# Norm steps of a two-layer decoder: one set of small operations for three token tiles, a shorter Newton step, a later fold, four lead units ahead of a norm

## The chip, the cores and the metric

The program runs on one core of one Trainium2 chip. Its metric is the time of one execution in microseconds on the device; the figures shown are the runs of the kernel before, and one further execution of it was profiled.

## The reference, cut to what matters

One inference step of a two-layer decoder with 1024 prompt tokens and 64 sample tokens (8 sequences of 8). Every layer is a mixer followed by a squared-ReLU MLP, and every one of these four sublayers has a norm in front and a norm behind:

```
def rmsnorm(x, g):
    xf = x.astype(jnp.float32)
    y = xf * lax.rsqrt(jnp.mean(xf * xf, axis=-1, keepdims=True) + EPS) * g.astype(jnp.float32)
    return y.astype(x.dtype)
...
    for l in range(DEPTH):
        h = rmsnorm(x, g_mix_pre[l])
        ...   # layer 0: m = pooling and short-convolution mixer; layer 1: m = (u * spatial(rmsnorm(v))) @ w_out_c
        x = x + rmsnorm(m, g_mix_post[l])
        h = rmsnorm(x, g_ffn_pre[l])
        f = jnp.square(jax.nn.relu(h @ w_up[l])) @ w_down[l]
        x = x + rmsnorm(f, g_ffn_post[l])
```

D_MODEL is 1024, the hidden size of the MLP 4096. Everything is float32.

## The kernel before, in words

**Products.** A float32 product is made of three products of rounded halves (`mm3`, L294 to L296): each operand is split into a rounded part and the rest (`hh` and `hl` of an activation, a cast on ACT at L116 and a subtraction on DVE at L117 of a weight tile `w` from its raw copy). Such three matmuls are called a triple here. A unit of an up projection is eight triples.

**Chunks.** The 1088 tokens are handled as three chunks: chunk 0 and chunk 1 of 384 prompt tokens (three tiles of 128), chunk 2 of 320 (256 prompt, 64 sample). Work runs over them in the order 2, 0, 1 (`ORD`). Chunk 2 is kept with features on the partitions, chunks 0 and 1 with tokens on the partitions.

**A boundary** is what lies between two sublayers: the norm behind, the residual add, the norm in front, and the halves `hh`, `hl` that the next products read. There are three boundaries in mid-program (here b1 at about 303 to 363 us between the first mixer and its MLP, b2 at about 1053 to 1113 us between that MLP and the second mixer, b3 at about 1386 to 1446 us between the second mixer and its MLP), a start that has only the norm in front, and a tail that has only the norm behind.

**Chunk 2's boundary** (`boundary`, `pre_tile`, `pre_end`): the sum of squares over partitions is made by a transposition on DVE, a reduction `red`, a matmul with a matrix `fold` on PE (`rstat`, L334 to L339), and a root with a Newton step (`rsqrt_small`). The first such fold belongs to the norm behind; after it eight tiles each are scaled (`acc`, L545, half on DVE and half on POOL), added to `x` (L554), split (`hh` L369 on ACT, `hl` L370 on DVE) and squared (L363 on ACT, L364 on POOL). The second fold (below: fold 2) gives the factor `rb` of the norm in front, which is applied only behind the up product (L878).

**Chunk 0's and chunk 1's boundary** (`boundary_tok`, `normed`): the sum of squares of the sublayer's output arrives in `ss` (squared on ACT at L470 as the last adds L467 are made); then for each of three token tiles: L431 adds two halves, `rsqrt_small` takes root and Newton step on a column of 128 x 1, L433 multiplies by it and the gain, L434 adds to `x`, ACT squares `x` with its sum (L415), a second `rsqrt_small` on 128 x 1, and ACT scales (L417). `arrive` then transposes the three tiles on PE (L454) and makes `hh` (L457, ACT) and `hl` (L458, DVE), eight of each.

**Order.** The boundaries are generators in a list `bg`; `pump(k)` advances it by k steps after each product (`E_STEPS` 3 in the last block of a sublayer, `U_STEPS` 7 between units), and a yielded number (`FOLD_GAP`) holds a generator until that many microseconds of products, by a count the program keeps, have been issued. A scheduler then fixes the order on each engine; each engine works its own list in that order. The last block of a sublayer has 24 triples of 512 columns for chunk 0 and 24 for chunk 1. The first four up units (`LEAD`, the lead units) are done for chunk 2, then for chunk 0, then for chunk 1. The rows of `x` that stay are written to memory by DMAs that ACT issues (L441), the outputs at the tail by DMAs that SP issues (L436).

## Time and profile before

| | us |
|---|---|
| three runs | 2178.21, 2180.25, 2180.49 (median 2180.25) |
| profiled execution | 2179.24 |
| its span | 2177.0 |
| PE busy | 2113.6 (97%) |
| DVE busy | 1275.7 (59%) |
| ACT busy | 689.5 (32%) |
| POOL busy | 73.0 (3%) |

The profiled execution lies 1.0 us under the median of the three runs, and its time is 2.2 us more than the span of its instructions. PE is TensorE's matmuls, DVE VectorE, ACT ScalarE, POOL GpSimd, SP SyncE. In a timeline row the first number is the start, the second the duration, and a bracket at the end gives the idle time just before and what ended it.

### The profile page before, as it was taken

To read this page: it belongs to the slowest core of one execution; us is meant where nothing else is said; L and a number is where in the kernel's file an instruction comes from. 1 tells how busy PE (TensorE), PEld (TensorE's weight loads), DVE (VectorE), ACT (ScalarE), POOL (GpSimd) and SP (SyncE) were. 2 spreads that over 40 slices of the span, in tenths; PEclk is the share of its full clock that TensorE was granted. 3 is DMA by queue.
4 is the path that set the end of the run, shared out by engine and by line. 5 is a ranking of instruction groups with operands and counts; after the bars stand their busy time and mean duration, and the time that the engine had idled before them with its cause. 6 is when DMAs were issued, how large, how long until landed. Compare 5 with 4: busy or idle time off the path is not lost.

```text
span 2177.0 us, 30946 instructions
## 1 busy us (share of the span) xinstructions
PE 2113.6 (97%) x12175; PEld 1985.4 (91%) x12175; DVE 1275.7 (59%) x2521; ACT 689.5 (32%) x1302; POOL 73.0 (3%) x93
## 2 busy tenths in 40 slices
PE   7999998999999999999999999989999999999997
PEld 6999988999999888888789999789999998888886
DVE  6536567966667345445673535678766663443456
ACT  7231236423234312112462221364222342220122
POOL 1000030000000000000300000300000000000000
PEclk9999999999999999999999999999999999999999
DMA  5111133332325233313122112333333352233222
GB/s 175 57 46 42 59 116 125 114 109 92 109 92 178 79 95 108 127 60 100 59 84 61 58 42 79 106 129 107 104 98 103 100 191 66 92 100 124 73 71 83
DMA packets 183605, 207.39 MB, mean 95 GB/s; under 512 B 10848, under 2 KB 154716, under 8 KB 181660
## 3 DMA queue, kind: packets, MB, share of 16 engines
q1 hardware_dynamic: 153644, 156.72, 22.9%
q10 hardware_dynamic: 29816, 48.69, 6.2%
q8 instruction: 96, 1.57, 0.3%
q14 instruction: 49, 0.40, 0.1%
HBM read 152.35 MB, written 53.14 MB: 94 GB/s over the span
## 4 chain that ended last, share of the span: by engine, by line
PE 91%; DVE 6%; DMA 1%; ACT 1%; issue 1%; SPq 0%; POOL 0%; ACTq 0%; DVEq 0%; POOLq 0%
PE ps L294 30%; PE ps L296 30%; PE ps L295 30%; DVE hl L370 1%; DVE x L554 1%; DVE acc L467 1%; PE aux L1157 1%; DVE x L434 1%; DVE acc L433 1%; DMA x<-in_x_prompt_dram 1%; DVE w L117 0%; DVE acc L545 0%; DVE hl L458 0%; DMA F<-fd 0%; DMA raw<-in_w_down_dram 0%
## 5 line engine op out<-in xcount | busy, mean ns | idle before, releaser
L294 PE MATMUL ps<-hh,w 128*128 128x384 f32 (+1 forms) x1696 | 553.6, 327 | 4.9 <-DVE hl L458 4.9
L296 PE MATMUL ps<-hh,w 128*128 128x384 f32 (+1 forms) x1696 | 550.3, 325 | 0.0
L295 PE MATMUL ps<-hl,w 128*128 128x384 f32 (+1 forms) x1696 | 550.1, 325 | 0.1
L116 ACT CAST w<-raw 128x512 fp32r<-128x512 f32 x404 | 248.9, 621 | 649.3 <-PE ps L296 572.8
L117 DVE TENSOR_TENSOR w<-raw,w 128x512 fp32r<-128x512 f32 x404 | 275.2, 688 | 147.8 <-ACT w L116 144.1
L294 PEld LDWEIGHTS ps<-hh,w 128*128 128x128 f32 x1696 | 319.9, 189 | 7.1 <-DVE hl L458 6.6
L295 PEld LDWEIGHTS ps<-hl,w 128*128 128x128 f32 x1696 | 320.1, 189 | 1.0 <-DVE hl L458 0.8
L296 PEld LDWEIGHTS ps<-hh,w 128*128 128x128 f32 x1696 | 319.8, 189 | 0.1
L467 DVE TENSOR_TENSOR acc<-ps,acc 128x512 f32<-128x512 f32 x240 | 164.7, 688 | 263.3 <-PE ps L296 263.2
L294 PE MATMUL ps<-w,F 128*128 128x512 f32 x720 | 281.7, 391 | 0.0
L296 PE MATMUL ps<-w,F 128*128 128x512 f32 x720 | 281.3, 391 | 0.0
L295 PE MATMUL ps<-w,F 128*128 128x512 f32 x720 | 281.2, 391 | 0.0
L296 PEld LDWEIGHTS ps<-w,F 128*128 128x128 f32 x720 | 135.7, 189 | 28.6
L295 PEld LDWEIGHTS ps<-w,F 128*128 128x128 f32 x720 | 135.7, 189 | 27.2
L294 PEld LDWEIGHTS ps<-w,F 128*128 128x128 f32 x720 | 135.7, 189 | 27.1
L968 DVE TENSOR_TENSOR f<-ps,f 128x384 f32<-128x384 f32 x182 | 101.0, 555 | 86.0 <-PE ps L296 80.2
L294 PE MATMUL ps<-F,w 128*128 128x320 f32 x480 | 148.3, 309 | 0.0
L296 PE MATMUL ps<-F,w 128*128 128x320 f32 x480 | 148.3, 309 | 0.0
L295 PE MATMUL ps<-F,w 128*128 128x320 f32 x480 | 148.3, 309 | 0.0
L493 DVE TENSOR_TENSOR acc<-ps,acc 128x320 f32<-128x320 f32 x160 | 76.9, 489 | 105.2 <-PE ps L296 104.1
L1029 ACT CAST F<-F 128x1536 fp32r<-128x1536 f32 (+3 forms) x48 | 64.1, 1335 | 206.4 <-DMA F<-fd 198.1
L295 PE MATMUL ps<-t,w 128*128 128x384 f32 x312 | 104.6, 335 | 0.0
(226 smaller groups left out, 3113.7 us busy)
## 6 DMA issues: line engine op xcount, KB each, us to landing
raw<-in_w_up_dram SPq DMA_DIRECT2D x128, 256.0 KB, 2.9
raw<-in_w_down_dram SPq DMA_DIRECT2D x128, 256.0 KB, 3.1
fd<-f ACTq DMA_DIRECT2D x120, 192.0 KB, 1.9
F<-fd SPq DMA_DIRECT2D x28, 768.0 KB, 4.6
fd<-f ACTq DMA_DIRECT2D x60, 160.0 KB, 1.9
xd<-x ACTq DMA_DIRECT2D x18, 512.0 KB, 2.6
x<-xd SPq DMA_DIRECT2D x6, 1536.0 KB, 8.8
F<-fd SPq DMA_DIRECT2D x14, 640.0 KB, 4.3
```

The lines of the kernel that those rows point to most:

```text
L116: nc.scalar.copy(out=wt[:, 0], in_=raw)
L117: nc.vector.tensor_tensor(out=wt[:, 1], in0=raw, in1=wt[:, 0].bitcast(F32), op=ALU.subtract)
L294: nc.tensor.matmul(out, lhsT=lh, rhs=rh, start=(j == 0), stop=False)
L295: nc.tensor.matmul(out, lhsT=lh, rhs=rl, start=False, stop=False)
L296: nc.tensor.matmul(out, lhsT=ll, rhs=rh, start=False, stop=(j == last))
L370: nc.vector.scalar_tensor_tensor(out=h[1][:, m, :], in0=x, scalar=gcol(g + m), in1=h[0][:, m, :].bitcast(F32), op0=ALU.mult, op1=ALU.subtract)
L433: nc.vector.scalar_tensor_tensor(out=acc[:, j], in0=acc[:, j], scalar=r, in1=GB[0], op0=ALU.mult, op1=ALU.mult)
L434: nc.vector.tensor_tensor(out=x[:, j], in0=x[:, j], in1=acc[:, j], op=ALU.add)
L467: nc.vector.tensor_tensor(out=acc, in0=v, in1=acc, op=ALU.add)
L493: nc.vector.tensor_tensor(out=acc[:, m, :], in0=ps, in1=acc[:, m, :], op=ALU.add)
L968: tt(out=out, in0=ps, in1=v, op=ALU.add)
L1029: nc.scalar.copy(out=f[:, :, 0, :], in_=f[:, :, 1, :].bitcast(F32))
```

## The change

- `rsqrt_small` has three fused operations behind root and reciprocal instead of five (a separate `v` is made only where it is needed).
- Chunks 0 and 1: the three tiles' sums are handled as one 128 x 3 column: one L451 add, one `rsqrt_small` for the norm behind, then for each tile the multiply, the add, and the square; one `rsqrt_small` for the norm in front; then the three scalings, of which the middle one is moved from ACT to DVE (L420). Before the first tile's scaling all three tiles must now be squared.
- `arrive` transposes tile by tile instead of feature by feature.
- `FOLD_GAP` is 12 instead of 6: a fold is placed after more products.
- The four lead units' products of chunk 2 are all issued before the kernel looks whether fold 2 has been placed; their results wait in PSUM.
- At the tail (`last`) the gain is multiplied in before the factor, the last operation and its output DMA are cut into two halves of 512 columns.

```diff
@@ -23,7 +23,7 @@
 PROMPT2 = 256
 NSLOT = 8
 E_STEPS = 3
-FOLD_GAP = 6.0
+FOLD_GAP = 12.0
 U_STEPS = 7
 WINDOWS = (2, 4, 8, 16)
 
@@ -315,17 +315,14 @@
 
     def rsqrt_small(src, n):
 
-        v = sm.tile([P, n], F32, name="v", tag="v")
         y = sm.tile([P, n], F32, name="y", tag="y")
         t = sm.tile([P, n], F32, name="t", tag="t")
         nc.scalar.activation(out=y, in_=src, func=AF.Sqrt, bias=eps_t)
-        nc.vector.tensor_scalar(out=v, in0=src, scalar1=EPS, scalar2=None, op0=ALU.add)
         nc.vector.reciprocal(out=y, in_=y)
-        nc.vector.tensor_tensor(out=t, in0=v, in1=y, op=ALU.mult)
-        nc.vector.tensor_tensor(out=t, in0=t, in1=y, op=ALU.mult)
-        nc.vector.tensor_scalar(out=t, in0=t, scalar1=-0.5, scalar2=1.5, op0=ALU.mult, op1=ALU.add)
-        nc.vector.tensor_tensor(out=y, in0=t, in1=y, op=ALU.mult)
-        return v, y
+        nc.vector.scalar_tensor_tensor(out=t, in0=src, scalar=EPS, in1=y, op0=ALU.add, op1=ALU.mult)
+        nc.vector.scalar_tensor_tensor(out=t, in0=t, scalar=-0.5, in1=y, op0=ALU.mult, op1=ALU.mult)
+        nc.vector.scalar_tensor_tensor(out=y, in0=t, scalar=1.5, in1=y, op0=ALU.add, op1=ALU.mult)
+        return y
 
     def rstat(ss, n, out, vtok=None, rtok=None):
 
@@ -337,11 +334,14 @@
         yield FOLD_GAP
         ap = aux()
         nc.tensor.matmul(ap[:, 0:nb], lhsT=fold, rhs=red[:, 0:nb], start=True, stop=True)
-        v, y = rsqrt_small(ap[:, 0:nb], nb)
+        y = rsqrt_small(ap[:, 0:nb], nb)
+        if vtok is not None:
+            v = sm.tile([P, nb], F32, name="v", tag="v")
+            nc.vector.tensor_scalar(out=v, in0=ap[:, 0:nb], scalar1=EPS, scalar2=None, op0=ALU.add)
         yield
         if out is not None:
             nc.vector.transpose(out=out, in_=y.unsqueeze(2).broadcast_to([P, nb, 32]))
-        for dst, src, last in ((vtok, v, 192), (rtok, y, 256)):
+        for dst, src, last in ((vtok, vtok is not None and v, 192), (rtok, y, 256)):
             if dst is None:
                 continue
             for a in range(4):
@@ -409,38 +409,58 @@
         GB[0] = mix_pool.tile([P, D], F32, name="gb", tag="mixa")
         nc.sync.dma_start(out=GB[0], in_=I[nm][layer:layer + 1, :].broadcast_to([P, D]))
 
-    def normed(c, j, v, junk, out):
-
-        ms = sm.tile([P, 1], F32, name="ms", tag="ms")
+    def square_sum(ms, v, junk):
         nc.scalar.activation(out=junk, in_=v, func=AF.Square, scale=1.0 / 32.0, accum_out=ms)
-        _, r = rsqrt_small(ms, 1)
-        nc.scalar.activation(out=out, in_=v, func=AF.Copy, scale=r)
+
+    def normed(c, ms):
+
+        r = rsqrt_small(ms, 3)
+        for j in range(3):
+            if j == 1:
+                nc.vector.tensor_scalar(out=ACC[c][:, j], in0=X[c][:, j], scalar1=r[:, j:j + 1], scalar2=None, op0=ALU.mult)
+            else:
+                nc.scalar.activation(out=ACC[c][:, j], in_=X[c][:, j], func=AF.Copy, scale=r[:, j:j + 1])
+        TOK[c] = True
 
     def begin_tok(c):
         ACC[c] = a_pool.tile([P, 3, D], F32, name=f"acc{c}", tag=f"acc{c}")
+        ms = sm.tile([P, 3], F32, name="ms", tag="ms")
         for j in range(3):
-            normed(c, j, X[c][:, j], ACC[c][:, j], ACC[c][:, j])
+            square_sum(ms[:, j:j + 1], X[c][:, j], ACC[c][:, j])
             yield
-        TOK[c] = True
+        normed(c, ms)
+        yield
 
     def boundary_tok(c, last):
         off = CH[c][0]
         x, acc = X[c], ACC[c]
+        if last:
+            for j in range(3):
+                nc.vector.tensor_tensor(out=acc[:, j], in0=acc[:, j], in1=GB[0], op=ALU.mult)
+                ms = sm.tile([P, 1], F32, name="ms1", tag="ms1")
+                nc.vector.tensor_tensor(out=ms, in0=SS1[c][:, j, 0:1], in1=SS1[c][:, j, 1:2], op=ALU.add)
+                r = rsqrt_small(ms, 1)
+                for h in range(2):
+                    cols = slice(h * 512, (h + 1) * 512)
+                    nc.vector.scalar_tensor_tensor(out=x[:, j, cols], in0=acc[:, j, cols], scalar=r, in1=x[:, j, cols],
+                                                   op0=ALU.mult, op1=ALU.add)
+                    nc.sync.dma_start(out=y_prompt[0, off + j * P:off + (j + 1) * P, cols], in_=x[:, j, cols])
+                yield
+            return
+        ms = sm.tile([P, 3], F32, name="ms", tag="ms")
+        nc.vector.tensor_tensor(out=ms, in0=SS1[c][:, :, 0], in1=SS1[c][:, :, 1], op=ALU.add)
+        r = rsqrt_small(ms, 3)
+        yield
+        ms2 = sm.tile([P, 3], F32, name="ms", tag="ms")
         for j in range(3):
-            ms = sm.tile([P, 1], F32, name="ms", tag="ms")
-            nc.vector.tensor_tensor(out=ms, in0=SS1[c][:, j, 0:1], in1=SS1[c][:, j, 1:2], op=ALU.add)
-            _, r = rsqrt_small(ms, 1)
-            nc.vector.scalar_tensor_tensor(out=acc[:, j], in0=acc[:, j], scalar=r, in1=GB[0], op0=ALU.mult, op1=ALU.mult)
+            nc.vector.scalar_tensor_tensor(out=acc[:, j], in0=acc[:, j], scalar=r[:, j:j + 1], in1=GB[0],
+                                           op0=ALU.mult, op1=ALU.mult)
             nc.vector.tensor_tensor(out=x[:, j], in0=x[:, j], in1=acc[:, j], op=ALU.add)
-            if last:
-                nc.sync.dma_start(out=y_prompt[0, off + j * P:off + (j + 1) * P, :], in_=x[:, j])
-                yield
-                continue
-            yield
-            normed(c, j, x[:, j], acc[:, j], acc[:, j])
+            square_sum(ms2[:, j:j + 1], x[:, j], acc[:, j])
             nc.scalar.dma_start(out=xd[c][:, j * D:(j + 1) * D], in_=x[:, j])
             yield
-        TOK[c] = True
+        normed(c, ms2)
+        yield
 
     def arrive(c, g):
 
@@ -449,8 +469,8 @@
         new_h(c)
         n = CH[c][1]
         pss = [psum() if m < 6 else aux() for m in range(KT)]
-        for m in range(KT):
-            for j in range(3):
+        for j in range(3):
+            for m in range(KT):
                 nc.tensor.transpose(pss[m][:, j * P:(j + 1) * P], ACC[c][:, j, m * P:(m + 1) * P], ident)
         for m in range(KT):
             v, (hh, hl) = pss[m][:, 0:n], H[c]
@@ -886,10 +906,9 @@
             else:
                 nc.scalar.dma_start(out=fd[c][:, j:j + 1, :], in_=stage[c][:, j % 2:j % 2 + 1, :])
 
-        def plain(j, c, w, normed=True):
-            ps = up_unit(w, c)
-            if not normed:
-                until_normed(c)
+        def plain(j, c, w, ps=None):
+            if ps is None:
+                ps = up_unit(w, c)
             if j % 2 == 0:
                 stage[c] = fslot(c, F32)
             squared(j, c, ps)
@@ -1000,11 +1019,18 @@
                 arrive(c, gup)
             if c == ORD[-1]:
                 bg.append(sums())
+            if c == 2:
+                pss = []
+                for w in lead:
+                    pss.append(up_unit(w, c))
+                    pump(U_STEPS)
+                until_normed(c)
             for j, w in enumerate(lead):
-                plain(j, c, w, j > 0 or c < 2)
+                plain(j, c, w, pss[j] if c == 2 else None)
                 if c == ORD[-1]:
                     W.done(w)
-                pump(U_STEPS)
+                if c < 2:
+                    pump(U_STEPS)
         for j in range(LEAD, PLAIN):
             w = take(1)[0]
             for c in range(NC):
@@ -1075,7 +1101,7 @@
             ve = sm.tile([P, 3], F32, name="ve", tag="ve")
             ts(out=ve, in0=VTOK[c], scalar1=EPS, scalar2=-EPS, op0=ALU.mult, op1=ALU.add)
             tt(out=ss, in0=ss, in1=ve, op=ALU.add)
-        _, rv = rsqrt_small(ss, 3)
+        rv = rsqrt_small(ss, 3)
         for j in range(3):
             ts(out=V[c][:, j, :], in0=V[c][:, j, :], scalar1=rv[:, j:j + 1], scalar2=None, op0=ALU.mult)
         if c == 2:
```

How the order of instructions moves is shown at b1, in three places. b2 and b3 have the same pattern.

PE around fold 2 of chunk 2 (`aux<-red,fold`; `ps<-w,f` and `ps<-w,fh` are products of the last block of chunk 1, `ps<-hh,w` those of chunk 2's lead units). Before:

```order
L294 MATMUL ps<-w,fh_2642 128x512
L295 MATMUL ps<-w,fh_2642 128x512
L296 MATMUL ps<-w,fh_2642 128x512
L339 MATMUL aux<-red,fold 128x10
L294 MATMUL ps<-w,f_2140 128x512
```

After:

```order
L295 MATMUL ps<-hl_2914,w 128x320
L296 MATMUL ps<-hh_2913,w 128x320
L336 MATMUL aux<-red,fold 128x10
L294 MATMUL ps<-hh_2913,w 128x320
L295 MATMUL ps<-hl_2914,w 128x320
```

Before, fold 2 stands between the sixteenth and the seventeenth of chunk 1's 24 triples; now it stands behind all of them and behind sixteen triples (two of four) of chunk 2's lead units. Fold 1 moves as well: it stood behind sixteen of chunk 0's 24 triples and stands now behind all 24.

DVE after the change, from the last steps of chunk 2's boundary to fold 2's root (`hl_2914` is chunk 2's `hl`, `acc_1312` chunk 1's sum, `red` what fold 2 multiplies, `y` of 128x10 chunk 2's factor and `y` of 128x3 chunk 0's):

```order
L370 SCALAR_TENSOR_TENSOR hl_2914<-x_2662,gains,hh_2913 128x320
L117 TENSOR_TENSOR w<-raw,w 128x512 x3
L574 SCALAR_TENSOR_TENSOR x_2662<-acc_1254,gains,x_2662 128x320
L487 TENSOR_TENSOR acc_1312<-ps,acc_1312 128x512 x2
L370 SCALAR_TENSOR_TENSOR hl_2914<-x_2662,gains,hh_2913 128x320
L487 TENSOR_TENSOR acc_1312<-ps,acc_1312 128x512
L117 TENSOR_TENSOR w<-raw,w 128x512
L331 STREAM_TRANSPOSE tmp<-f_2818 128x320
L333 TENSOR_REDUCE red<-tmp 128x10
L117 TENSOR_TENSOR w<-raw,w 128x512 x3
L321 RECIPROCAL y<-y 128x10
L321 RECIPROCAL y<-y 128x3
```

Before, the same place reads (`v`, `y` of 128x10 are chunk 2's):

```order
L467 TENSOR_TENSOR acc_1365<-ps,acc_1365 128x512
L334 STREAM_TRANSPOSE tmp<-f_2871 128x320
L336 TENSOR_REDUCE red<-tmp 128x10
L467 TENSOR_TENSOR acc_1365<-ps,acc_1365 128x512
L117 TENSOR_TENSOR w<-raw,w 128x512 x3
L322 TENSOR_SCALAR v<-aux 128x10
L323 RECIPROCAL y<-y 128x10
```

Four weight splits L117 stand now ahead of `red` in chunk 2's last steps, and chunk 0's factor has come to stand behind fold 2's root in one run with it.

DVE around chunk 0's first `hl` (`x_2658` and `acc_1287` are chunk 0's, `x_2660` and `acc_1312` chunk 1's, `hl_3301` is chunk 0's `hl`). After:

```order
L420 TENSOR_SCALAR acc_1287<-x_2658,y 128x1024
L324 SCALAR_TENSOR_TENSOR y<-t,y 128x3
L456 SCALAR_TENSOR_TENSOR acc_1312<-acc_1312,y,gb 128x1024 x2
L458 TENSOR_TENSOR x_2660<-x_2660,acc_1312 128x1024 x2
L456 SCALAR_TENSOR_TENSOR acc_1312<-acc_1312,y,gb 128x1024
L458 TENSOR_TENSOR x_2660<-x_2660,acc_1312 128x1024
L321 RECIPROCAL y<-y 128x3
L322 SCALAR_TENSOR_TENSOR t<-ms,y 128x3
L323 SCALAR_TENSOR_TENSOR t<-t,y 128x3
L324 SCALAR_TENSOR_TENSOR y<-t,y 128x3
L420 TENSOR_SCALAR acc_1312<-x_2660,y 128x1024
L478 SCALAR_TENSOR_TENSOR hl_3301<-ps,gains,hh_3300 128x384
```

Before (chunk 1's are `acc_1365` and `x_2713`, chunk 0's `hl` is `hl_3464`):

```order
L327 TENSOR_TENSOR y<-t,y 128x1
L433 SCALAR_TENSOR_TENSOR acc_1365<-acc_1365,y,gb 128x1024
L434 TENSOR_TENSOR x_2713<-x_2713,acc_1365 128x1024
L458 SCALAR_TENSOR_TENSOR hl_3464<-ps,gains,hh_3463 128x384
L431 TENSOR_TENSOR ms<-ss_3019 128x1
L458 SCALAR_TENSOR_TENSOR hl_3464<-ps,gains,hh_3463 128x384 x2
```

Before, chunk 0's first `hl` follows the first of chunk 1's three tiles; now it follows all three and chunk 1's scaling. On ACT the same: chunk 0's first `hh` (`hh_3300`) follows the last of chunk 1's three squares and its root, its second follows chunk 1's two scalings:

```order
L413 ACTIVATE acc_1312,ms<-x_2660 128x1024
L460 DMA xd_228<-x_2660 128x1024
L320 ACTIVATE y<-ms,eps_t 128x3
L907 DMA fd_232<-f_3293 128x320
L477 ACTIVATE hh_3300<-ps,gains 128x384
L422 ACTIVATE acc_1312<-x_2660,y 128x1024 x2
L477 ACTIVATE hh_3300<-ps,gains 128x384 x5
```

## Rows read from the trace of the kernel before

**Rows 1.** Page, part 1: busy time, share of span, instructions of each engine.

```profile
PE 2113.6 (97%) x12175; PEld 1985.4 (91%) x12175; DVE 1275.7 (59%) x2521; ACT 689.5 (32%) x1302; POOL 73.0 (3%) x93
```

**Rows 2.** Waits of PE: total us, times, longest us.

```profile
PE ps L454 <- ACT acc L417: 18.6, 9, 4.2
PE aux L339 <- DVE red L336: 14.7, 3, 5.1
...
PE ps L294 <- DVE hl L458: 5.7, 7, 3.3
```

**Rows 3.** Timeline of PE at b1.

```profile
303.58 0.28 PE L339 MATMUL aux<-red,fold 128*128 128x10 f32 x2
...
325.08 0.60 PE L339 MATMUL aux<-red,fold 128*128 128x10 f32 x2 [4.75 <-DVE red L336]
...
357.62 0.69 PE L294 MATMUL ps<-hh,w 128*128 128x384 f32 x1 [0.22 <-DVE hl L458]
```

**Rows 4.** Windows at b1: length, PE, PEld, DVE, ACT, POOL busy, PE clock, DMA.

```profile
326.00:332.00 6.00, 6.00 (x19) 4.70 (x19) 3.10 (x16) 0.74 (x3) 0.00 (x0) 0.65 0.46 131
356.00:362.00 6.00, 5.78 (x23) 5.38 (x22) 5.93 (x21) 5.77 (x12) 0.00 (x0) 0.59 0.21 87
```

**Rows 5.** Timeline of DVE at b1.

```profile
305.52 0.51 DVE L343 STREAM_TRANSPOSE f<-y 128x320 f32<-128x320 f32 x1
306.07 1.58 DVE L545 TENSOR_TENSOR acc<-acc,f 128x320 f32<-128x320 f32 x2
...
324.53 0.49 DVE L336 TENSOR_REDUCE red<-tmp 128x10 f32<-128x320 f32 x1
...
325.54 1.89 DVE L117 TENSOR_TENSOR w<-raw,w 128x512 fp32r<-128x512 f32 x3
...
334.68 1.28 DVE L433 SCALAR_TENSOR_TENSOR acc<-acc,y,gb 128x1024 f32<-128x1024 f32 x1
...
356.96 0.61 DVE L458 SCALAR_TENSOR_TENSOR hl<-ps,gains,hh 128x384 fp32r<-128x384 f32 x1
```

**Rows 6.** Groups by line, DVE and ACT: count | busy us, mean ns | idle.

```profile
L433 DVE SCALAR_TENSOR_TENSOR acc<-acc,y,gb 128x1024 f32<-128x1024 f32 x24 | 30.8, 1283 | 0.6
...
L434 DVE TENSOR_TENSOR x<-x,acc 128x1024 f32<-128x1024 f32 x24 | 29.3, 1219 | 0.3
...
L417 ACT ACTIVATE acc<-x,y 128x1024 f32<-128x1024 f32 x24 | 27.4, 1147 | 7.3 <-DVE y L327 5.9 <-DVE t L326 1.4
...
L415 ACT ACTIVATE acc<-x 128x1024 f32<-128x1024 f32 x24 | 25.5, 1061 | 16.3 <-DVE x L434 12.2 <-DMA x<-in_x_prompt_dram 2.6 <-DVE ms L431 1.4
...
L325 DVE TENSOR_TENSOR t<-t,y 128x1 f32<-128x1 f32 x48 | 7.5, 158 | 0.1
...
L1080 DVE TENSOR_SCALAR v<-v,y 128x1024 f32<-128x1024 f32 x9 | 6.2, 750 | 0.1
```

**Rows 7.** Timeline of POOL, then of DVE, inside chunk 2's tiles at b1.

```profile
313.03 5.73 POOL L364 TENSOR_TENSOR f<-f,tmp 128x320 f32<-128x320 f32 x5 [2.48 <-ACT tmp L363]
...
312.75 0.53 DVE L554 SCALAR_TENSOR_TENSOR x<-acc,gains,x 128x320 f32<-128x320 f32 x1
...
313.62 1.17 DVE L554 SCALAR_TENSOR_TENSOR x<-acc,gains,x 128x320 f32<-128x320 f32 x1
```

**Rows 8.** Timeline of PE at b2.

```profile
1075.91 0.57 PE L339 MATMUL aux<-red,fold 128*128 128x10 f32 x2 [5.09 <-DVE red L336]
...
1108.67 0.58 PE L294 MATMUL ps<-w,hh 128*128 128x256 f32 x1 [0.22 <-DVE hl L458]
```

**Rows 9.** Timeline of the start, PE and ACT.

```profile
22.01 0.69 PE L294 MATMUL ps<-hh,w 128*128 128x384 f32 x1 [3.33 <-DVE hl L458]
...
17.84 1.15 ACT L417 ACTIVATE acc<-x,y 128x1024 f32<-128x1024 f32 x1
```

**Rows 10.** Tail: last DVE row of the timeline; output DMAs, us to landing.

```profile
2172.18 1.22 DVE L434 TENSOR_TENSOR x<-x,acc 128x1024 f32<-128x1024 f32 x1
...
out_dram<-x SPq DMA_DIRECT2D x6, 512.0 KB, 2.6
```

## The prediction

> **What bounds the kernel now.** The page's first part comes first: PE is busy 97% of the span, the next engine 59% [rows 1]. So only what happens while PE stands still can pay, and the list of PE's waits says what that is: 18.6 us for ACT's scaling of chunks 0 and 1 (L417), 14.7 us in three waits for chunk 2's `red` (fold 2, once in each of b1, b2, b3), 5.7 us for the first `hl` of a chunk [rows 2]. Together 39 us, 1.8% of the time. The rest cannot be reached by an edit of norms, except through the clock: after such a wait the granted clock falls. In the six microseconds behind fold 2's wait at b1 it is 0.65, in the six behind the wait for the transposed chunk 0 it is 0.59 [rows 4], so some 2 us more go with each long wait. What decides at a boundary is therefore not DVE's or ACT's busy share, but two dates: when PE has fold 2, and when chunk 0's first `hl` is there, since from then on PE has work without a gap. At b1 these are 325.08 and 357.62 us [rows 3]. I replay b1 with the order after the change and the durations before, then take b2, b3, start and tail from it.
>
> **Fold 1 is later.** From fold 1 at 303.58 to the end of what stood ahead of fold 2 (325.08 less its wait of 4.75 = 320.33) PE did 24 triples of 512 columns [rows 3]: 0.698 us each. Fold 1 moves behind eight more: +5.5, to about 309.1. The order then puts chunk 0's sixth square ahead of its root on ACT, and chunk 1's first add ahead of the transposition of its result on DVE. That add needs chunk 1's first four triples, 309.1 + 0.1 + 2.8 = 312.0, and takes 0.7; the transposition takes 0.5 [rows 5]. The first scaling (L545 before) starts at about 313.2 instead of 306.07 [rows 5]: 7.1 late. DVE has nothing of this chain to do meanwhile.
>
> **The chain from there to `red`.** Before, it ran from 306.07 to 325.02, the end of the reduction [rows 5]: 18.95 us, with DVE busy throughout, adds of chunk 1 among it. After, four weight splits stand ahead of `red` too, at 0.63 each (three in 1.89) [rows 5]: +2.5. So `red` is ready at 313.2 + 18.95 + 2.5 = 334.6, where before it was 325.0.
>
> **What PE does meanwhile.** Its 24 triples of chunk 1 end at 309.1 + 0.1 + 16.7 = 325.9, and the two lead units that now stand ahead of fold 2 are 16 triples of 320 columns, by columns 0.44 each, 7.0 us: fold 2 would be wanted at 332.9. But the lead units read chunk 2's last `hl` and weights whose splits stand in the same DVE list, some six operations ahead of `red`. I take the three splits done at about 328.7, the last `hl` at 332.3. So PE waits some 3 us for weights and again for `hl`, finishes unit 1 at 332.7 and unit 2 at 336.2; with a spell of lower clock as in [rows 4], of which 1.6 us fall into unit 2, fold 2 goes at 337.8 (from 334.9, no lower clock and nothing late but `red`, up to 338.5). The 4.75 us of fold 2's wait are gone as such, and stand again as waits of unit 1. Before, eight triples of chunk 1 and four units were left behind fold 2; now two units are, so PE is not behind. Chunk 0 is.
>
> **Chunk 0's norm.** Its factor stands in one run with fold 2's. Root, reciprocal, twice three small steps of about 0.16 [rows 6] and the transposition make 1.9: the first multiply L456 goes at 339.7 instead of 334.68 [rows 5]. Then chunk 0 is quicker than before, because nothing of ACT stands between its tiles: three times 1.28 + 1.22 [rows 6], less 0.1 overlap at each, plus one split, 7.7, to 347.4. The last square and its sum are 1.25 [rows 6], root and four small steps 0.95: factor at 349.6. The middle tile's scaling moves to DVE; no such row exists, the nearest is L1080, the same operation on the same shape, 0.75 [rows 6] (bounds 0.75 to 1.28): 350.4. ACT's two scalings end at about 352, PE's transpositions by 354.
>
> **And then it waits for chunk 1.** In DVE's new order all of chunk 1's boundary stands between that and chunk 0's first `hl`: 7.1 us of multiplies and adds, 1.25 last square, 0.95 root and steps, 0.75 scaling, from 350.5 to 360.5; `hl` 0.61 [rows 5], to 361.2. Before it stood behind chunk 1's first tile only. Chunk 0's first product starts at about 361.3 instead of 357.62: **+3.7**. Behind it `hh` 2 waits for ACT's two scalings of chunk 1 (2 × 1.15 [rows 6]) and the other `hl` follow one each 0.53, so unit 1 ends at about 367.2 against 363.4 (eight triples of 0.52, 1.6 lost to the clock): I take **+4.2 for b1**, bounds +2.3 and +6. Only if fold 2 goes before 334.9 is the new order better than the old.
>
> **b3** is b1 again, +4.2. **b2**: fold 2 waited until 1075.91 and chunk 0's first product began at 1108.67 [rows 8]. The same replay (lead products of 256 columns, so even less work covers the chain) gives fold 2 at 1086.5 to 1088 and the first product at 1110.3 to 1112.5, its unit's end 2.5 to 6 late: **+4**.
>
> **Start.** Before, each tile's root followed its own square and the last scaling ended at 18.99; PE's first real product came at 22.01 [rows 9]. Now three squares run first, one root serves all, and the middle scaling is DVE's; by the same durations the first product comes at about 18.8. But chunk 1's first `hl` is then ready only at about 46, a microsecond after PE wants it: **−2.4** (−1 to −4).
>
> **Tail.** The last add now starts behind a smaller run of small steps and in halves, and its output is half as large; before, it started at 2172.18 and ended at 2173.40, and an output of 512 KB took 2.6 [rows 10]. About 0.6 on DVE and 0.4 of DMA: **−1** (0 to −1.6).
>
> The fused Newton step saves one small operation on each path, 0.16; it is contained above.
>
> **Sum.** 4.2 + 4 + 4.2 − 2.4 − 1.0 = +9.0 on 2179.24, 2188.2; the profiled execution lies 1.0 under the median of its runs, so the time to expect is **2189**. With the bounds of every term at once it would be 2179.24 + 1.0 + (2.3 + 2.5 + 2.3 − 4 − 1.6 = +1.5) to (18 − 1 = +17): 2182 to 2197. A measurement tells 0.2%, 4.4 us, from no change.
>
> **Rival 1, faster: DVE keeps up.** If chain and splits are done when PE wants fold 2, it goes at 332.9, and every date before 334.9 decides for this rival; chunk 0's first product comes 4.9 earlier than in my replay, at 356.4, 1.2 ahead of before. Three boundaries gain 0.7 to 1.2 each, start and tail 3.4: 2174. If the clock's spells go with the waits, 2 us each, 2168. For it: 60 small operations of 0.16 go from DVE at each boundary [rows 6], and nine rows of the chain are stretched while POOL adds: the same L554 takes 0.53 alone and 1.17 beside POOL's run [rows 7]; without POOL the chain would be 5.4 shorter, and `red` ready at 329.2. Against it: the small operations lie behind fold 2, not in the chain, and POOL's adds are started by the same tiles, so they move with them. [...] Chance 0.2.
>
> **Rival 2, no change.** If fold 2 goes at about 335, each boundary costs about 1, and start and tail give it back: 2180. The bound of `red` alone is 334.6, so this needs only that unit 1's weights come some 3 us earlier than I place them. Chance 0.17.
>
> **Rival 3, worse.** Every wait of unit 1, of the transpositions and of chunk 0's `hl` brings its own spell of half clock, 2 us each in place of one: 2194 to 2200. Chance 0.08. My own forecast, 2184.6 to 2194, keeps 0.55.
>
> So faster 0.2, same 0.17, slower 0.63. Range for 8 in 10: 2172 (rival 1 with half its clock gain) to 2198.
>
> **What would show it.** PE's waits: the three for `red` shrink under 1 us each or vanish, and new ones appear at L294 for DVE's splits or for chunk 2's `hl` just before fold 2, and a wait of 7 us or so for chunk 0's `hl`, in place of 4.2 for ACT's scaling. Fold 2 near 337 us at b1 and chunk 0's first product near 361 (its own clock aside). The first product of the program near 18.8. I am wrong if PE's first lead unit starts at 326 without a wait, or if chunk 0's first `hl` is ready before 357: then the chain ran faster than before's rows say.

## The result and the profile after

The changed kernel takes 2195.67 us (median of four runs, 2194.71 to 2199.59) against 2179.72 for the kernel before (four runs): a ratio of 1.0075, 95% interval 1.0063 to 1.0087, slower by some 16 us. It lies in the range; the direction was right, and the forecast was 9 us. The profiled execution of the changed kernel is the slowest of its four: 2199.59 us, span 2197.9.

The page's first part, as [rows 1] before:

```profile
PE 2119.0 (96%) x12175; PEld 1991.7 (91%) x12175; DVE 1256.0 (57%) x2294; ACT 674.2 (31%) x1266; POOL 72.5 (3%) x93
```

DVE has 227 instructions fewer and is 19.7 us less busy, ACT 15.3: the small operations did go. PE does the same matmuls in 5.4 us more, so some of them ran at a lower clock (mean granted clock 0.984, before 0.988), and of the 20.9 us that the span grew the other 15.5 are PE's idle time. The list of PE's waits says where, beside [rows 2]:

```profile
PE ps L474 <- ACT acc L422: 21.5, 4, 7.3
PE ps L294 <- DVE hl L478: 17.8, 7, 6.2
...
PE ps L296 <- DVE w L117: 6.5, 2, 3.2
PE ps L295 <- DVE w L117: 4.3, 3, 2.1
PE ps L474 <- DVE work L729: 2.5, 1, 2.5
```

The 14.7 us for `red` are gone. In their place stand 10.8 us for weight splits; the wait for a chunk's first `hl` has grown from 5.7 to 17.8, and that for ACT's scalings from 18.6 to 21.5. PE at b1, the same places as [rows 3]:

```profile
307.79 0.28 PE L336 MATMUL aux<-red,fold 128*128 128x10 f32 x2
...
328.07 0.47 PE L296 MATMUL ps<-hh,w 128*128 128x320 f32 x1 [3.24 <-DVE w L117]
...
336.45 0.28 PE L336 MATMUL aux<-red,fold 128*128 128x10 f32 x2
...
351.23 1.54 PE L474 MATMUL ps<-ident,acc 128*128 128x128 f32 x6 [7.35 <-ACT acc L422]
...
361.77 0.69 PE L294 MATMUL ps<-hh,w 128*128 128x384 f32 x1 [5.60 <-DVE hl L478]
```

PE waits three times here: at the first lead unit for weights, for chunk 0's scaling, for chunk 0's first `hl`. DVE at b1, to be read beside [rows 5]: first scaling of chunk 2, three weight splits, `red`, chunk 0's first multiply, the last add of chunk 1, chunk 0's first `hl`.

```profile
312.12 1.58 DVE L565 TENSOR_TENSOR acc<-acc,f 128x320 f32<-128x320 f32 x2
...
327.34 1.88 DVE L117 TENSOR_TENSOR w<-raw,w 128x512 fp32r<-128x512 f32 x3
...
333.87 0.49 DVE L333 TENSOR_REDUCE red<-tmp 128x10 f32<-128x320 f32 x1
...
340.02 1.24 DVE L456 SCALAR_TENSOR_TENSOR acc<-acc,y,gb 128x1024 f32<-128x1024 f32 x1
...
356.87 1.23 DVE L458 TENSOR_TENSOR x<-x,acc 128x1024 f32<-128x1024 f32 x1
...
361.11 0.61 DVE L478 SCALAR_TENSOR_TENSOR hl<-ps,gains,hh 128x384 fp32r<-128x384 f32 x1
```

And ACT between fold 2 and its root:

```profile
337.47 0.62 ACT L116 CAST w<-raw 128x512 fp32r<-128x512 f32 x1 [2.67 <-DMA raw<-in_w_up_dram]
337.99 0.26 ACT L320 ACTIVATE y<-aux,eps_t 128x10 f32<-128x10 f32 x1
```

A cast that waits for a weight's DMA stands ahead of the root in ACT's list, so fold 2, issued at 336.45, is taken up by the root only at 337.99; before, the root followed fold 2 by 0.64 us (325.72 behind 325.08).

Where the time went is read from the same PE products in both traces, as the distance of their starts: around a boundary the order of products differs, between boundaries it is the same and the distance stands still. The changed kernel is 1.2 us ahead in front of b1, 5.0 us behind after it, 9.9 after b2 and 20.6 after b3; 0.9 more is lost at some 1809 us, and the tail gives 0.6 back. Between b2 and b3 it loses 2.6 us at a place that none of the edits touches, where PE waits for POOL's step on a weight of the mixer (first row before, second changed):

```profile
1153.69 0.66 PE L1115 MATMUL aux<-ident,sp_raw 128*128 128x128 f32 x4 [1.40 <-POOL sp_raw L1111]
```

```profile
1164.62 1.11 PE L1141 MATMUL aux<-ident,sp_raw 128*128 128x128 f32 x4 [2.47 <-POOL sp_raw L1137]
```

The granted clock is 0.57 from 1164 to 1168 us there, and 1.00 from 1153 to 1156 before. In e2 and e8 below, which are as late at this place, the wait is 1.3 and 1.4 us, so these 2.6 us are not shown to belong to the change. The boundaries themselves cost 6.2 (b1), 4.9 (b2) and 8.2 (b3) in this execution, which is 4 us longer than the median of the four.

### The profile page after: what moved, and what is told of

Its sections match the earlier page's. It is cut to its first block, busy times and chain, and to the rows that moved or that the text cites. A ratio compares the mean times of both kernels' runs of the same rounds, so it can differ in the third digit from the quotient of the medians.

```text
span 2197.9 us, 30693 instructions
## 1 busy us (share of the span) xinstructions
PE 2119.0 (96%) x12175; PEld 1991.7 (91%) x12175; DVE 1256.0 (57%) x2294; ACT 674.2 (31%) x1266; POOL 72.5 (3%) x93
## 4 chain that ended last, share of the span: by engine, by line
PE 44%; DVE 4%; DMA 1%; ACT 1%; issue 0%; DVEq 0%; POOL 0%; SPq 0%; POOLq 0%; ACTq 0%
PE ps L294 14%; PE ps L295 14%; PE ps L296 14%; DVE acc L456 1%; PE aux L1183 1%; DVE x L458 1%; DVE w L117 0%; DVE x L445 0%; DVE acc L487 0%; DVE x L574 0%; DVE hl L370 0%; DMA F<-fd 0%; DMA raw<-in_w_up_dram 0%; DMA sp_raw<-in_w_spatial_dram 0%; DMA raw<-in_w_uv_dram 0%
## 5 line engine op out<-in xcount | busy, mean ns | idle before, releaser
L117 DVE TENSOR_TENSOR w<-raw,w 128x512 fp32r<-128x512 f32 x404 | 275.1, 688 | 151.6 <-ACT w L116 148.0
```

Source lines behind the costliest of these rows:

```text
L117: nc.vector.tensor_tensor(out=wt[:, 1], in0=raw, in1=wt[:, 0].bitcast(F32), op=ALU.subtract)
```

## The experiments

Each was timed in the same session as the kernel before, whose median was between 2179.8 and 2181.5. The changed kernel stands at 1.0075. "Changed" and "before" name the kernel that an edit starts from.

**e1, the fold gap back at 6** (changed).

```
-FOLD_GAP = 12.0
+FOLD_GAP = 6.0
```

> The changed kernel with the fold gap back at 6, all else as changed. Theory (the fold gap puts chunk 2's chain 6 us later and with it fold 2 and chunk 0's norm): fold 1 and fold 2 stand where they stood before, fold 2 waits some 4.7 us again, chunk 0's first multiply comes at about 333 us at b1, its first product at about 352 instead of 361.8. Three boundaries some 9 us quicker than in the changed kernel: about 2168 us (2162 to 2175), faster than before. Rival (the cost lies in the one set of small operations, whose three tiles wait for each other): still above 2188.

2173.73 us, ratio 0.9968 (0.9955 to 0.9980): 22 us under the changed kernel and 7 under the kernel before. PE waits for fold 2 again, and yet chunk 0's first product is ten microseconds earlier than at 361.77:

```profile
321.48 0.60 PE L336 MATMUL aux<-red,fold 128*128 128x10 f32 x2 [4.43 <-DVE red L333]
...
351.52 0.69 PE L294 MATMUL ps<-hh,w 128*128 128x384 f32 x1 [0.76 <-DVE hl L478]
```

So the one set of operations is no loss by itself, and the gap is. In the profiled execution 3.3 us of what it gains on the kernel before lie at the start, 1.0 at the tail and 2.8 at the three boundaries together.

**e2, lead units not ahead of the norm** (changed): `until_normed` is called after the first lead unit again, the results are used one by one.

```
...
-            if c == 2:
-                pss = []
-                for w in lead:
-                    pss.append(up_unit(w, c))
-                    pump(U_STEPS)
-                until_normed(c)
             for j, w in enumerate(lead):
-                plain(j, c, w, pss[j] if c == 2 else None)
+                plain(j, c, w, None, c == 2 and j == 0)
...
-                if c < 2:
-                    pump(U_STEPS)
+                pump(U_STEPS)
```

> The changed kernel with the lead units not ahead of the norm: the place of fold 2 is asked for after the first lead unit as before, fold gap 12. Theory: fold 2 waits for red anyway (334.4 at b1), so it goes only some 2 us earlier than 336.5; 2 us less per boundary, about 2190 us (2186 to 2194). Rival (the lead units ahead are the cost, since they wait for weights and delay fold 2): all of the loss goes, 2180.

2193.22 us, ratio 1.0056 (1.0043 to 1.0068). Some 2 us of the loss, as expected, though the interval still overlaps that of the changed kernel (1.0063 to 1.0087): PE then waits 2.43 us for `red` at b1 instead.

**e3, chunk 1's boundary held back** (changed).

```
-            bg.append(boundary_tok(c, gpre is None))
+            if gpre is not None and c == ORD[-1]:
+                held.append(boundary_tok(c, False))
+            else:
+                bg.append(boundary_tok(c, gpre is None))
...
     def arrive(c, g):
...
+        while held and c == ORD[1]:
+            bg.append(held.pop())
```

> The changed kernel, but chunk 1's boundary is put into the queue only when chunk 0's transpositions and halves have been issued. Theory (chunk 0's first hl waits behind chunk 1's whole boundary): fold 2 stays at about 336.5 at b1, chunk 0's first product comes at about 354.5 instead of 361.8; 5 to 7 us less per boundary, about 2178 us (2173 to 2184). Rival (what counts is fold 2's date alone, chunk 1's boundary would be waited for later): 2192 to 2196.

2172.05 us, ratio 0.9964 (0.9951 to 0.9976): 24 us under the changed kernel and below the 2173 to 2184 that I gave. Fold 2 goes at 335.93, as late as ever, and chunk 0's first `hl` starts at 356.54 instead of 361.11, its products with it:

```profile
335.93 0.29 PE L336 MATMUL aux<-red,fold 128*128 128x10 f32 x2
...
357.20 0.45 PE L294 MATMUL ps<-hh,w 128*128 128x384 f32 x1 [1.39 <-DVE hl L478]
```

**e4, gap 6 and the hold together** (changed).

> Both: fold gap 6 and chunk 1's boundary held back. Theory: fold 2 waits 4.7 us as before, chunk 0's hl is ready when the lead units of chunk 2 end, first product of chunk 0 at about 350 us at b1 instead of 357.6 before; three times 7 us under the kernel before, plus start and tail: about 2158 us (2153 to 2167). Rival (only one of the two counts at a time): as the better one of the two, about 2168.

2158.99 us, ratio 0.9900 (0.9885 to 0.9915): 14.7 under e1 and 13.1 under e3. As expected: both edits count, each less once the other is made. What is left on PE is mostly fold 2, three waits, of which the one at b2 is put down to `ms`:

```profile
PE aux L336 <- DVE red L333: 9.0, 2, 4.5
PE ps L294 <- DVE hl L478: 5.6, 7, 1.8
PE aux L336 <- DVE ms L451: 4.7, 1, 4.7
```

**e5, gap 6 for the first fold and 12 for the second** (changed): `rstat` gets its gap as an argument.

```
-    def rstat(ss, n, out, vtok=None, rtok=None):
+    def rstat(ss, n, out, vtok=None, rtok=None, gap=12.0):
...
-        yield FOLD_GAP
+        yield gap
...
-        yield from rstat(ss1, n, rb1)
+        yield from rstat(ss1, n, rb1, gap=6.0)
```

> The changed kernel with a gap of 6 for the first fold of chunk 2 and 12 for the second. Chunk 2's chain starts as before, fold 2 stands behind all 24 triples of chunk 1 and PE has no wait for it. Theory (chunk 0's first hl, behind chunk 1's boundary, sets the end; fold 2's wait on PE is cover): chunk 0's first product at about 351 us at b1 as in the run with the gap at 6, so about 2171 us (2166 to 2177), no better than that run (2173.7). Rival (PE's waits for fold 2 are what counts): 4.5 us of wait and 2 of lower clock go at each of three boundaries, about 2154.

2173.91 us, ratio 0.9970 (0.9959 to 0.9981), the same as e1. PE has no wait for fold 2 any more (13.6 us in e1), and it stands still later instead:

```profile
323.91 0.28 PE L336 MATMUL aux<-red,fold 128*128 128x10 f32 x2
...
344.78 1.54 PE L474 MATMUL ps<-ident,acc 128*128 128x128 f32 x6 [6.42 <-ACT acc L422]
...
355.32 0.69 PE L294 MATMUL ps<-hh,w 128*128 128x384 f32 x1 [6.08 <-DVE hl L478]
```

I had expected the first product at 351; it came at 355.3, since chunk 0's first multiply came at 333.56 and not at 328: three weight splits more had moved ahead of fold 2's root. The sum hides two opposite things. Against e1, e5 loses 4.0 us at b1 and 2.9 at b3, where chunk 0's first multiply comes 4.0 and 3.4 us later, and gains 6.4 at b2, where it comes 2.8 earlier (all counted from the distance in front of the boundary). And e5 differs from the changed kernel in the first fold's gap alone: 22 us come back by it, so what costs in the later gap is fold 1, with which chunk 2's chain begins.

**e6, the two gaps and the hold** (changed; edits of e3 and e5).

> The same two gaps, 6 and 12, with chunk 1's boundary held back. Theory: now fold 2's wait is on the path, since chunk 0's hl no longer is; fold 2 goes at about 324 without a wait, chunk 2's lead units end near 339, chunk 0's first product comes at about 344 instead of 351.1; some 6 us less at each boundary than in the run with gap 6 and the hold (2159): about 2142 us (2136 to 2152). Rival (DVE's list cannot serve chunk 0 earlier than there): 2155 to 2160.

2151.66 us, ratio 0.9867 (0.9854 to 0.9881): 7.3 under e4, the fastest of all. By boundary it gains 3.5 (b1), 6.0 (b2) and 0.6 us (b3) on e4: with chunk 0's `hl` not behind chunk 1, no boundary loses by the wait's going any more. Less than the 17 expected, because chunk 0's norm is now the bound, at b1 and b3 (6.3 us of wait each):

```profile
324.57 0.28 PE L336 MATMUL aux<-red,fold 128*128 128x10 f32 x2
...
345.34 1.54 PE L474 MATMUL ps<-ident,acc 128*128 128x128 f32 x6 [6.31 <-ACT acc L422]
...
350.74 0.44 PE L294 MATMUL ps<-hh,w 128*128 128x384 f32 x1 [1.10 <-DVE hl L478]
```

In both profiled executions PE idles 50.1 us; what falls is its busy time, from 2108.2 to 2099.3 us, with a mean granted clock of 0.994 against 0.992. At b1 the transpositions behind the wait of 6.31 us are slow at first, six in 1.54 us, and then faster, six in 0.82; chunk 0's first product, behind a wait of 1.10 us, takes 0.44 us. In e5, behind a wait of 6.08, it takes 0.69.

**e7, gap 6 and lead units not ahead** (changed; edits of e1 and e2).

> The changed kernel with gap 6 and the lead units not ahead of the norm: of the change only the one set of operations, the shorter Newton step, the tail and the order of transpositions are left. Theory: with the gap at 6 the folds stand at the same places with and without it, so the lead units ahead are worth nothing there: 2173.7 as with gap 6 alone, within 2.5. Rival (lead units ahead save a look at the norm on PE): 2178 or more.

2173.13 us, ratio 0.9968 (0.9956 to 0.9981): as e1. With the gap at 6 the lead units ahead of the norm are worth nothing; the 7 to 8 us under the kernel before come from what is left. In the profiled execution 3.4 of them lie at the start, 1.0 at the tail and 2.2 at the three boundaries; what each of the remaining edits does there was not taken apart.

**e8, gap 12 alone** (before).

```
-FOLD_GAP = 6.0
+FOLD_GAP = 12.0
```

> The kernel before with the gap at 12 and nothing else. Theory: fold 2's date moves from 325 to about 335 at b1, but only the first tile of chunk 1 stands ahead of chunk 0's hl, so chunk 0's first product comes some 2 us late: about 2187 us (2182 to 2193). Rival (a later fold alone explains all of the change's loss): 2195 or more. Second rival (a wait of PE removed is time gained): under 2176.

2199.86 us, ratio 1.0090 (1.0076 to 1.0104). My 2187 was wrong and the first rival right: in the old kernel too the gap costs 18 us, as much as the whole change. In the profiled execution 17.6 us of it lie at the boundaries and 3.0 at the tail. ACT's list shows what I had left out: chunk 2's and chunk 0's roots stand behind a cast that waits for its weight,

```profile
339.17 0.62 ACT L116 CAST w<-raw 128x512 fp32r<-128x512 f32 x1 [2.52 <-DMA raw<-in_w_up_dram]
339.70 0.27 ACT L321 ACTIVATE y<-aux,eps_t 128x10 f32<-128x10 f32 x1
```

3.7 us behind fold 2, which goes at 335.99, so the first multiply comes at 342.01, where the kernel before has 334.68. From there the old norm's three tiles go one after the other through DVE, ACT and DVE, and PE waits for each scaling in turn:

```profile
349.64 0.88 PE L454 MATMUL ps<-ident,acc 128*128 128x128 f32 x6 [2.61 <-ACT acc L417]
...
357.03 1.54 PE L454 MATMUL ps<-ident,acc 128*128 128x128 f32 x6 [6.13 <-ACT acc L417]
...
362.41 1.54 PE L454 MATMUL ps<-ident,acc 128*128 128x128 f32 x6 [3.41 <-ACT acc L417]
...
364.60 0.69 PE L294 MATMUL ps<-hh,w 128*128 128x384 f32 x1 [0.22 <-DVE ms L431]
```

**e9, chunk 0's boundary in a queue of its own** (e6): `last_block` puts chunk 0's `boundary_tok` into a second queue, which `pump` serves while the first is held by a fold gap.

```
-        while k > 0 and bg and (force or pe[0] >= pe[1]):
+        while k > 0 and (bg or beside):
+            if bg and (force or pe[0] >= pe[1]):
...
+            elif beside:
+                try:
+                    next(beside[0])
+                    k -= 1
+                except StopIteration:
+                    beside.popleft()
+            else:
+                break
```

> The run with gaps 6 and 12 and the hold, and chunk 0's boundary in a queue of its own, so that it need not wait for the place of fold 2. Theory: there chunk 0's norm sets the end of each boundary (PE waits 6.3 us for its scaling at b1 and b3), since its first multiply stands behind fold 2's root and that behind three weight splits; now it goes right behind red, at about 324 instead of 333 at b1, and chunk 0's first product at about 344 instead of 350.7: about 2140 us (2133 to 2148). Rival (the results of the lead units keep the PSUM banks that chunk 0's transpositions need until fold 2's factor is there, so nothing is won): 2149 to 2154.

2159.77 us, ratio 0.9907 (0.9894 to 0.9921): 8 slower than e6. Neither reading was right. Chunk 0's multiplies do start at 324.46, and now they stand ahead of the lead units' weight splits on DVE:

```profile
324.60 0.41 PE L305 MATMUL ps<-hh,w 128*128 128x320 f32 x1 [0.37 <-DVE w L117]
...
331.06 0.63 PE L305 MATMUL ps<-hh,w 128*128 128x320 f32 x1 [4.15 <-DVE w L117]
...
349.49 0.44 PE L303 MATMUL ps<-hh,w 128*128 128x384 f32 x1 [1.30 <-DVE hl L487]
```

What chunk 0 won, the lead units lost. Most of the loss against e6, 6.4 us, is at b2, where a lead unit waits 4.28 us for a split.

**e10, the same with gap 9 for fold 2** and chunk 1 released one lead unit later.

```
-    def rstat(ss, n, out, vtok=None, rtok=None, gap=12.0):
+    def rstat(ss, n, out, vtok=None, rtok=None, gap=9.0):
...
     def arrive(c, g):
...
-        while held and c == ORD[1]:
-            bg.append(held.pop())
+        if held and c == ORD[1]:
+            cool[0] = 1
...
     def pump(k, force=False):
...
+        if held and cool[0]:
+            cool[0] -= 1
+            if not cool[0]:
+                bg.append(held.pop())
```

> The same with fold 2 four triples earlier (gap 9) and chunk 1's boundary held until chunk 0's first lead unit is issued. Theory: fold 2 waits some 1.6 us for red, the lead units' results leave PSUM earlier, chunk 0's transpositions with them; within 4 us of the run before it, 2136 to 2144. Rival (any wait for fold 2 costs its length and a spell of lower clock, 2 to 3 us at each boundary): 2147 to 2150.

2155.63 us, ratio 0.9890 (0.9875 to 0.9905): above both the 2136 to 2144 and the rival's 2147 to 2150. Four below e9, but two things differ between them, and which of them gave it is not shown; PE waits 1.73 us for `red` and 2.73 for a split at b1.

**e11, the fused Newton step alone** (before): `v` is made behind the step, and only for columns of more than three.

```
-        nc.vector.tensor_scalar(out=v, in0=src, scalar1=EPS, scalar2=None, op0=ALU.add)
         nc.vector.reciprocal(out=y, in_=y)
-        nc.vector.tensor_tensor(out=t, in0=v, in1=y, op=ALU.mult)
-        nc.vector.tensor_tensor(out=t, in0=t, in1=y, op=ALU.mult)
-        nc.vector.tensor_scalar(out=t, in0=t, scalar1=-0.5, scalar2=1.5, op0=ALU.mult, op1=ALU.add)
-        nc.vector.tensor_tensor(out=y, in0=t, in1=y, op=ALU.mult)
+        nc.vector.scalar_tensor_tensor(out=t, in0=src, scalar=EPS, in1=y, op0=ALU.add, op1=ALU.mult)
+        nc.vector.scalar_tensor_tensor(out=t, in0=t, scalar=-0.5, in1=y, op0=ALU.mult, op1=ALU.mult)
+        nc.vector.scalar_tensor_tensor(out=y, in0=t, scalar=1.5, in1=y, op0=ALU.add, op1=ALU.mult)
+        if n > 3:
+            nc.vector.tensor_scalar(out=v, in0=src, scalar1=EPS, scalar2=None, op0=ALU.add)
```

> The kernel before with the fused Newton step alone. Theory: one small operation less, 0.2 us, in each of six roots of chunk 0's chain at a boundary, not all of it on the path: 2 to 4 us, about 2177.5 (2175 to 2181). Rival (the small operations are what bounds the boundaries): 2172 or less.

2178.62 us, ratio 0.9993 (0.9984 to 1.0002): no difference that this measurement can tell from none; of the 2 to 4 us that I gave, 2 lie just inside the interval and 4 outside.

**e12, the hold alone** (before; edit of e3).

> The kernel before with chunk 1's boundary held back as in the run with the hold, nothing else. Theory: with a root for each tile chunk 1's first tile alone stands ahead of chunk 0's hl and fits into a wait for ACT; holding the rest back is worth under 1 us a boundary: 2179 (2176 to 2182). Rival (chunk 1's work ahead of chunk 0's hl costs in this kernel too): 15 us less, as between the runs with gap 6, 2166.

2184.42 us, ratio 1.0018 (1.0010 to 1.0027). Slightly slower, outside the 2176 to 2182 that I gave: what is held back arrives later in its turn, and PE waits for chunk 1's third tile, at b1 and by as much at b3. Its waits for ACT's scalings are 20.7 us in all against 18.6; the rest was not taken apart.

```profile
377.68 0.88 PE L454 MATMUL ps<-ident,acc 128*128 128x128 f32 x6 [0.98 <-ACT acc L417]
```

So at the old gap the hold pays only together with the one set, and there it pays 15 to 24 us (e4 against e1, e3 against the changed kernel).

**The runs by boundary.** Microseconds lost (+) or won (-) against the kernel before at each place, from one profiled execution each, read like the distances above. What lies elsewhere is left out; it is under 1 us but for the changed kernel's 2.6 and 0.9.

| | start | b1 | b2 | b3 | tail |
|---|---|---|---|---|---|
| changed | -1.2 | +6.2 | +4.9 | +8.2 | -0.6 |
| e1, gap 6 | -3.3 | -2.1 | +0.1 | -0.8 | -1.0 |
| e3, hold | -1.6 | -0.6 | -2.8 | -1.1 | -0.6 |
| e4, gap 6 and hold | -1.7 | -4.3 | -4.6 | -6.6 | -1.0 |
| e5, gaps 6 and 12 | -1.7 | +1.9 | -6.3 | +2.2 | -0.6 |
| e6, gaps 6 and 12, hold | -1.0 | -7.8 | -10.6 | -7.2 | -0.6 |
| e8, gap 12 alone | 0.0 | +7.0 | +4.0 | +6.6 | +3.0 |

## Why the prediction was right, and where it was off

Dates of the prediction are on the time axis of the kernel before. The changed kernel comes to b1 1.23 us ahead, so a date measured there has to be taken 1.23 us later before it is held against a forecast.

**Fold 1 and chunk 2's chain.** Right. Forecast: first scaling at 313.2, end of `red` at 334.6. Measured: 312.12 and 334.36, on the forecast's axis 313.4 and 335.6.

**What PE does meanwhile.** Right in the main. PE was to wait some 3 us for weights at the first lead unit: 3.24, and the three splits end at 329.2 where I had 328.7. The second wait that I gave the lead units, for chunk 2's last `hl`, did not come. Fold 2 went at 336.45, on the forecast's axis 337.7 (337.8). The wait for `red` is gone from the list and stands there as waits for L117.

**From fold 2 to chunk 0's first multiply.** Too short: 3.6 us and not 1.9. That the date looks right, 340.02 against 339.7, is luck, since the start's gain hides the difference: on the forecast's axis it is 341.3. What I had left out is a cast on ACT that waits for a weight's DMA ahead of the root, and behind it the split of that weight on DVE ahead of the reciprocal (338.12 to 338.7); e8 has the same cast.

**Chunk 0's first `hl` behind chunk 1's boundary.** The mechanism is right, and the date again by luck: forecast end 361.2 and product at 361.3, measured 361.72 and 361.77, on the forecast's axis 363.0. The signs that I named were half right: PE waits 5.6 us there and not 7, and its wait for ACT's scaling just before, which I had said would make room for it, has grown from 4.2 to 7.35. e3 shows chunk 1's place as a cause: with fold 2 as late as ever, taking chunk 1's work out of the way brings back all of the loss and 8 us more. e5 against e1, and e6 against e4, remove PE's waits for fold 2 (13.6 us in e1), without the hold and with it. Without it b1 and b3 lose, with it they gain; b2 gains 6 us either way.

**What the gap costs.** The prediction said that only a fold 2 before 334.9 makes the new order better than the old. e1 agrees, at 321.48 and 7 us under the kernel before. e8 and e5 add what it did not say: the gap alone costs 18 us with the old norm and 22 with the new, and with the new norm all 22 come from the first fold's gap. So the change is a loss of some 20 from one number, less a gain from the rest: 7 us at gap 6, some 3 at gap 12, where the intervals of e8 and the changed kernel overlap.

**The size of the boundaries** is the mis-sized term: 4.2, 4 and 4.2 against 6.2, 4.9 and 8.2 in the profiled execution. That is 6.9 of the 11.9 us by which its growth of 20.9 exceeds the forecast of 9; 2.6 are the wait for `sp_raw` and 0.9 the place at 1809, for which I had no term, 1.2 the start and 0.4 the tail. Two things are in the boundaries. First, chunk 0's first product is 5.4 us late at b1 and 6.0 at b3, each against the distance in front of that boundary, and not 3.7; at b1 the first multiply is already 1.6 late, by the cast and the split. Second, the clock: I gave chunk 0's first unit the same spell of lower clock as before, 1.6 us of loss. At b3 it lasts longer behind that unit's start. Before, PE's granted clock was 0.51 from 1440 to 1443 us and then 1.00; after, behind a wait of 6.21 us that ended at 1458.70, it was 0.50 from 1458 to 1464:

```profile
1440.00:1443.00 3.00, 2.78 (x10) 2.76 (x10) 2.97 (x16) 2.78 (x8) 0.00 (x0) 0.51 0.43 175
1443.00:1446.00 3.00, 3.00 (x19) 3.00 (x18) 2.96 (x7) 2.33 (x4) 0.00 (x0) 1.00 0.00 0
```

```profile
1458.00:1461.00 3.00, 2.25 (x5) 1.38 (x6) 2.15 (x5) 3.00 (x6) 0.00 (x0) 0.50 0.00 0
1461.00:1464.00 3.00, 3.00 (x10) 3.00 (x11) 2.82 (x6) 1.85 (x4) 0.00 (x0) 0.50 0.00 0
1464.00:1467.00 3.00, 3.00 (x16) 3.00 (x16) 0.06 (x1) 0.49 (x1) 0.00 (x0) 0.85 0.00 0
```

The first fence is the kernel before, the second the changed one (columns as in [rows 4]). In the first row of the second, PE is busy 2.25 of 3 us with five matmuls, because `hh` 2 waits for ACT's two scalings of chunk 1, as forecast. The whole of PE's busy time grew by 5.4 us. That is the third rival, with 0.08: its 2194 to 2200 is where the time fell, 2195.67, just above the 2184.6 to 2194 that I held likeliest. At b1 its mechanism is seen: the granted clock is 0.50 in or behind each of PE's three waits (328.3 to 331.7, 348.8 to 355.5 and 359.1 to 365.8 us), before in or behind two (323.4 to 330.2 and 354.1 to 360.9). But it explains 5.4 of 20.9 us, and the other 15.5 are waits.

**Start and tail.** The first product came at 18.55 (forecast 18.8). But PE then stood 2.5 us at chunk 1's transpositions, where I had given a microsecond, and not for `hl` but for DVE's L729, which reads a PSUM tile.

```profile
18.55 0.44 PE L294 MATMUL ps<-hh,w 128*128 128x384 f32 x1 [0.28 <-DVE hl L478]
...
44.13 0.88 PE L474 MATMUL ps<-ident,acc 128*128 128x128 f32 x6 [2.52 <-DVE work L729]
```

So 1.2 us gained and not 2.4; behind that wait the granted clock is 0.50 from 45 to 48 us. In the other runs with the new start the same distance is 1.0 to 3.4 us. The tail gave 0.6 and not 1.

**Rival 1** (DVE keeps up) fell at its own condition: fold 2 went after 334.9. Its argument from the number of small operations fell with it. In the changed kernel 227 instructions fewer on DVE saved 19.7 us of its busy time and none of the program's; at gap 6 the same gathering stands in a kernel 7 us faster, with 2 to 3 us of that at the boundaries (e1, e7), and the Newton step alone (e11) moves nothing that can be told. Gathering does save time on DVE: in the changed kernel's trace the three fused operations of a root take 0.15 us each on a column of one and 0.16 on a column of three. At these boundaries that time was not on the path that decides.

**Open.** How much of the 18 to 22 us of the gap belongs to the cast that waits for its weight, and how much to the later fold as such, was not tested. In the changed kernel the root stands 1.5, 1.7 and 0.6 us behind fold 2 at the three boundaries, before 0.6, 2.6 and 0.6, so there the wait at the root is the small part; in e8 it stands 3.5 to 3.7 us behind. Why PE's clock stays at 0.50 for over 5 us behind chunk 0's first product at b3 (to 1464 and beyond) and for 4 at b1 (to 365.8), and why the changed kernel's four runs spread over 5 us, is not shown either.

## What to carry to other kernels

Removing a wait of the busiest engine pays only if nothing later at the same boundary becomes the bound: in e5 13.6 us of waits for a fold went without a gain in sum, won at one boundary and lost at two, and in e6 their going paid. Look at each boundary, since a sum over them can hide both. Before a step is moved later, list what is queued behind it on every engine that it feeds; here chunk 0's norm, not the fold's own reader, was what came late. And gathering three tiles into one set pays most when the order lets the first set through: at gap 6 it paid 7 us with the next chunk's whole set ahead of the first chunk's use (e1), and 22 with that set held back (e4).

## What the runs showed of the hardware

PE's first instruction, which waits for the first DMAs, came between 8.9 (e9) and 11.2 us (e6) in the profiled executions of kernels that load the same data first, so up to some 2 us of a difference at the start need not be of the kernel. And a wait of PE in mid-run can be paid twice: in e9 a lead unit's matmul behind a wait of 4.15 us for a weight takes 0.63 us and those that follow 0.47, where the one of the same shape behind a wait of 0.37 takes 0.41 and those that follow 0.31. In the changed kernel matmuls of this shape take 0.47 us at a granted clock of 0.50 (328.3 to 331.2 us, behind a wait of 3.24) and 0.31 at 1.00 (331.7 to 333.0). In e6 at b1 chunk 0's first product pays less, 0.44 us against 0.69 in e5, with a wait of 1.10 us just before it in place of 6.08.
